# A delta rule with masked exponents and masked copies, unpadded convolutions and packed Fourier tables, in a two-block network on one core

## The chip, the cores and the metric

The kernel runs on one core of one Trainium2 chip. The metric is the device time in microseconds (us). Three runs of the kernel before took 3624.77, 3631.09 and 3634.4 us; their median, 3631.09 us, is the time before.

## The reference, cut to what matters

The program is two networks behind one another, for 512 positions of width 1024, in fp32. Each has two layers. A layer of the first network has two feed-forward parts and a mixer whose outputs are concatenated: latent attention, an mLSTM (with a depthwise convolution of 5 taps) and a Fourier mixer. A layer of the second network has one feed-forward part and a mixer of sliding-window attention, a gated linear recurrence and the gated delta rule (with a depthwise convolution of 4 taps). The change touches three places.

The Fourier mixer takes the real part of a 2-D transform over positions and group channels, and maps it per group:

```
zg = z.reshape(B, S, 4, 64)
y = fftn(zg, axes=(1, 3), norm='ortho').real
out = einsum('bsgc,gce->bsge', y, w).reshape(B, S, 256) + b
```

The delta rule works on chunks; g is a cumulative sum inside a chunk, and T is the inverse of a unit lower triangular matrix:

```
G = cumsum(gc, axis=-1)
L = exp(where(incl, G[..., :, None] - G[..., None, :], -inf))
kb = kc * bc[..., None]
A = where(strict, einsum('bnhtd,bnhsd->bnhts', kb, kc) * L, 0.0)
T = triangular_solve(eye + A, eye, lower=True, unit_diagonal=True)
U = T @ (vc * bc[..., None]);  W = T @ (kb * exp(G)[..., None])
qk = where(incl, einsum('bnhtd,bnhsd->bnhts', qc, kc) * L, 0.0)
# then, chunk after chunk:
v_new = u - w @ state
o = qd @ state + qkc @ v_new
state = gl * state + kd.T @ v_new
```

The convolutions are depthwise, over positions, with zeros outside the sequence: 5 taps centred in the first network, 4 taps that look back in the second, each followed by a SiLU.

## The kernel before, in words

Activations lie with channels on the 128 partitions and the 512 positions along the row. Weights come from HBM in pieces of 128x1024 (512 KB) on SyncE's (SP's) queue, in the order in which they are used. Each is cut into a high and a low part, ScalarE (ACT) writing the high one (line 382) and VectorE (DVE) the low one (line 383), and a product is three matmuls (lines 407 to 409). The weight parts live in two pools of four buffers each, `whi` and `wlo`; a raw piece in a pool of three, `wraw`. PSUM tiles of 128x512 come from two pools of four, `mm` and `mx`.

The program is written as Python generators. `weave` takes a step of each in turn, and the program's order of instructions on each engine follows from that and from a scheduler behind it, which moves instructions by costs of its own. On the chip each engine works its list in order.

In the second network's mixer the order is: gated recurrence with the first projections, then sliding-window attention up to its keys, the six convolutions (their projection's weights are the last to fill `whi` and `wlo`), and then `weave(gdn, swa)`: the delta rule and the attention, step by step, both wanting PE, DVE and ACT. The attention goes by four pairs of heads: scores (line 1127), mask and maximum (1130, 1132), four small operations (1137 to 1140), 8 exponents on ACT (1144), a division by the sum (1146, 1147, 1149), transposes (1164), a copy (1166), values (1173).

The delta rule goes by four blocks of 128 positions (`block`), each for four heads at once, so its tiles are 128x512. For each block: differences of the cumulative sums `ge` (1443) and their exponent (1444); GpSimd (POOL) multiplies that by a strict mask (1448, into `es`); k times k (1452), times beta and `es` (1454, into `am`). POOL masks `am` to its first off-diagonal (1457), DVE subtracts that from the identity (1458, into `xx`), PE transposes it (1461) and ACT copies it (1462, into `xt`). POOL masks `ge` inclusively (1464), for q times k (1467, 1468), which is transposed (1472, 1473). Then come six rounds that double the inverted size: POOL masks `am` to the round's off-diagonal blocks (1479, `gao`), PE multiplies it with `xt` (1482), ACT copies (1483, `zt`), PE multiplies `xx` with that (1487), DVE subtracts it from `xt` (1488), PE transposes (1493) and ACT copies (1494, new `xx`). `es`, `xt`, `am` and `zt` lie in one `whi` and one `wlo` buffer per block.

In the Fourier mixer, `z` is multiplied with a cosine and a sine table of 257 columns each (line 1057: 4 matmuls per table and half of the channels, 2056 bytes of table per partition in each of 4 transfers), copied (1058), and combined with small products (1060, 1061, 1063) in lines 1068 and 1069. The convolution (`conv`) copies its input into a tile of 520 columns whose margins it clears (832, 834), multiplies with the first tap (840) and adds the others (842).

## Time and profile before

| | |
|---|---|
| median of 3 runs | 3631.09 us |
| the profiled execution | 3626.56 us |
| its span, first to last instruction | 3624.7 us |
| PE (matmuls) busy | 3515.3 us, 97% |
| DVE busy | 2015.2 us, 56% |
| ACT busy | 1370.3 us, 38% |
| POOL busy | 239.2 us, 7% |
| mean granted TensorE clock | 0.989 of full speed |

How to read it: a busy PE is not a PE at its peak, since matmuls are pipelined and their ends modelled. L12 is line 12 of the kernel. An arrow in a row reads "output <- inputs"; behind it stand the tile's shape and the number of instructions. "Idle before <- releaser" says how long the engine sat idle in front of a group and what ended that. The chain of waits is followed back from the last instruction; it names at each moment the one engine that the end waited for. The granted clock is a share of 2.4 GHz; 0.5 is the lower of its two levels.

### The profile page before, as it was taken

The numbers are of one execution on the slowest core, as the hardware profiler recorded it, in microseconds if no ns is written. First come the engines' busy times: TensorE is split into PE (matmuls) and PEld (weight loads), VectorE is DVE, ScalarE is ACT, GpSimd is POOL, SyncE is SP. The second block draws the span as 40 slices with busy tenths as digits, with TensorE's granted clock in tenths as the row PEclk, the third lists the DMA queues.
The fourth block names the chain that finished last, engine by engine and source line by source line (L and its number), as shares of the span: only waits on it lengthen the run. The fifth ranks groups of instructions, "written<-read, shape, count | busy, mean of one in ns | idle before, by whom it ended". The sixth has DMA issues, their size and how long they took to land.

```text
span 3624.7 us, 44757 instructions
## 1 busy us (share of the span) xinstructions
PE 3515.3 (97%) x17726; PEld 2914.2 (80%) x17726; DVE 2015.2 (56%) x3084; ACT 1370.3 (38%) x2247; POOL 239.2 (7%) x202
## 2 busy tenths in 40 slices
PE   9999999999999999999999999899999989899999
PEld 7888778888888888778888887688888877788887
DVE  6555665554575545664555676856333476654333
ACT  4223354223342223463223373454222453543221
POOL 0000000000000000000000002430000022500000
PEclk9999999999999999999999999899999999999999
DMA  5443202444424443213444221002333221022332
GB/s 166 143 132 124 86 29 79 134 145 129 127 93 151 134 148 95 77 39 93 140 145 131 92 78 55 25 14 75 105 94 103 77 66 43 1 71 88 101 96 82
DMA packets 105952, 344.75 MB, mean 95 GB/s; under 512 B 11408, under 2 KB 19600, under 8 KB 105744
## 3 DMA queue, kind: packets, MB, share of 16 engines
q1 hardware_dynamic: 105744, 341.89, 29.7%
q8 instruction: 140, 2.29, 0.3%
q14 instruction: 68, 0.56, 0.0%
HBM read 339.75 MB, written 2.10 MB: 94 GB/s over the span
## 4 chain that ended last, share of the span: by engine, by line
PE 84%; DVE 7%; issue 5%; ACT 2%; POOL 1%; DMA 0%; SPq 0%; POOLq 0%; DVEq 0%; ACTq 0%
PE mm L407 24%; PE mm L409 24%; PE mm L408 24%; PE mm L1487 1%; PE mm L1482 1%; PE mm L478 1%; PE mx L969 1%; PE mm L476 1%; PE mm L477 1%; ACT sc L1144 1%; DVE wlo L383 1%; PE mm L810 1%; PE mx L949 1%; DVE sc L1149 1%; DVE hacc L1285 1%
## 5 line engine op out<-in xcount | busy, mean ns | idle before, releaser
L382 ACT CAST whi<-wraw 128x1024 fp32r<-128x1024 f32 (+3 forms) x540 | 552.9, 1028 | 1570.7 <-PE mm L408 1278.7
L407 PE MATMUL mm<-xh,whi 128*128 128x512 f32 (+1 forms) x2784 | 1053.3, 380 | 8.8 <-ACT whi L382 6.3
L408 PE MATMUL mm<-xl,whi 128*128 128x512 f32 (+1 forms) x2784 | 1055.8, 380 | 1.6 <-DVE xl L589 1.5
L409 PE MATMUL mm<-xh,wlo 128*128 128x512 f32 (+1 forms) x2784 | 1055.6, 380 | 0.4 <-DVE wlo L383 0.3
L383 DVE TENSOR_TENSOR wlo<-wraw,whi 128x1024 fp32r<-128x1024 f32 (+3 forms) x540 | 643.1, 1193 | 275.9 <-ACT whi L382 234.0
L407 PEld LDWEIGHTS mm<-xh,whi 128*128 128x128 f32 x2784 | 522.1, 188 | 107.3 <-ACT whi L382 6.3
L409 PEld LDWEIGHTS mm<-xh,wlo 128*128 128x128 f32 x2784 | 524.9, 189 | 100.8 <-DVE wlo L383 3.3
L408 PEld LDWEIGHTS mm<-xl,whi 128*128 128x128 f32 x2784 | 525.0, 189 | 100.3 <-DVE xl L589 2.4
L409 PE MATMUL mm<-hi,wlo 128*128 128x512 f32 (+1 forms) x1390 | 537.5, 387 | 2.1 <-DVE wlo L383 2.1
L407 PE MATMUL mm<-hi,whi 128*128 128x512 f32 (+1 forms) x1390 | 538.6, 388 | 0.2
L408 PE MATMUL mm<-lo,whi 128*128 128x512 f32 (+1 forms) x1390 | 537.5, 387 | 0.0
L409 PEld LDWEIGHTS mm<-hi,wlo 128*128 128x128 f32 x1390 | 261.1, 188 | 61.0 <-DVE wlo L383 4.2
L407 PEld LDWEIGHTS mm<-hi,whi 128*128 128x128 f32 x1390 | 260.9, 188 | 57.3 <-ACT hi L400 1.1
L408 PEld LDWEIGHTS mm<-lo,whi 128*128 128x128 f32 x1390 | 261.1, 188 | 55.9
L659 DVE SCALAR_TENSOR_TENSOR h<-mm,h 128x512 f32<-128x512 f32 x112 | 77.1, 690 | 237.9 <-PE mm L409 237.9
L1595 DVE SCALAR_TENSOR_TENSOR ada<-wraw,cond,ada 128x1024 f32<-128x1024 f32 x84 | 107.8, 1283 | 95.6 <-DMA wraw<-in_ada_w_dram 95.1
L638 DVE TENSOR_TENSOR gl<-mm,rstd 128x512 f32<-128x512 f32 x88 | 60.7, 690 | 154.3 <-PE mm L409 154.3
L637 DVE TENSOR_TENSOR silu<-mm,rstd 128x512 f32<-128x512 f32 x88 | 60.7, 689 | 143.4 <-PE mm L409 143.3
L659 DVE SCALAR_TENSOR_TENSOR h<-mm,mod,h 128x512 f32<-128x512 f32 (+1 forms) x70 | 48.9, 704 | 153.6 <-PE mm L409 153.6
L400 ACT CAST hi<-gl 128x512 fp32r<-128x512 f32 x132 | 82.0, 621 | 103.3 <-DVE gl L640 102.6
L634 DVE TENSOR_TENSOR gl<-silu,mm 128x512 f32<-128x512 f32 x44 | 30.2, 687 | 135.2 <-PE mm L409 135.2
L401 DVE TENSOR_TENSOR lo<-gl,hi 128x512 fp32r<-128x512 f32 x132 | 90.4, 685 | 15.7 <-ACT hi L400 15.7
(498 smaller groups left out, 3761.0 us busy)
## 6 DMA issues: line engine op xcount, KB each, us to landing
wraw<-in_ffn_gate_dram SPq DMA_DIRECT2D x130, 512.0 KB, 3.5
wraw<-in_ffn_up_dram SPq DMA_DIRECT2D x130, 512.0 KB, 4.1
wraw<-in_ada_w_dram SPq DMA_DIRECT2D x96, 512.0 KB, 3.7
wraw<-in_ffn_down_dram SPq DMA_DIRECT2D x96, 448.0 KB, 3.3
wraw<-in_win_f_dram SPq DMA_DIRECT2D x50, 512.0 KB, 3.5
wraw<-in_ffn_down_dram SPq DMA_DIRECT2D x48, 512.0 KB, 3.5
wraw<-in_w_out_dram SPq DMA_DIRECT2D x32, 512.0 KB, 3.5
wraw<-in_win_t_dram SPq DMA_DIRECT2D x16, 512.0 KB, 3.4
```

The lines of the kernel that those rows point to most:

```text
L382: self.nc.scalar.copy(hi[:, s], raw)
L383: self.nc.vector.tensor_tensor(lo[:, s], raw, hi[:, s].bitcast(F32), op=ALU.subtract)
L400: self.nc.scalar.copy(hi, src)
L401: self.nc.vector.tensor_tensor(lo, src, hi.bitcast(F32), op=ALU.subtract)
L407: T.matmul(ps, whi, xhi, start=first, stop=False)
L408: T.matmul(ps, whi, xlo, start=False, stop=False)
L409: T.matmul(ps, wlo, xhi, start=False, stop=last)
L476: T.matmul(ps, xh[:, bs], w[0][:, s], start=k == 0, stop=False)
L637: nc.vector.tensor_tensor(sg, gate_ps, rb, op=ALU.mult)
L638: nc.vector.tensor_tensor(gg, up_ps, rb, op=ALU.mult)
L659: self.nc.vector.scalar_tensor_tensor(h, ps[:, c], scale, h, op0=ALU.mult, op1=ALU.add)
L1595: V.scalar_tensor_tensor(acc, raw, cond[:, k:k + 1], acc, op0=ALU.mult, op1=ALU.add)
```

## The change

Fourier tables: cosines and sines go side by side into one table of 512 columns (257 cosines, 255 sines; the first and last sine column, both zero, are dropped), so each half of the channels needs 4 matmuls of 512 columns, one copy of 512 columns, and one copy of two small products together. The convolution starts with the tap that needs no shift over all 512 columns, and adds each other tap only over the columns where its input exists, so that no margin is kept or cleared. With both, the tiles of the `m` and `l` slots are 2048 bytes per partition; their numbers (16 and 17) stay.

In the delta rule the POOL multiplications go. The exponent's argument is the maximum of the difference and a mask that holds 0 on and below the diagonal and 1e30 above it, so that its exponent is already masked inclusively. `am` is made with minus beta. `xx` and `xt` begin as identities, which a DMA on SP's queue writes from the identity in SBUF into the `whi` buffer of the block (128 partitions, 8 pieces of 512 bytes each). The first off-diagonal is copied over them through a mask by DVE, once from SBUF and once from PSUM. In each round PE multiplies the whole of `am` with `xt`, and DVE copies only the masked part of the product over `xt`.

```
-    m["strict"] = c < r
-    m["incl"] = c <= r
-    for h in LEVELS[::-1]:
-        m[f"off{h}"] = m[f"lv{h}"].T
+    m["later"] = np.where(c <= r, 0.0, -NEG)
+    m["off1"] = m["lv1"].T
...
-    both = np.stack([np.cos(ang), np.sin(ang)])
-    return np.ascontiguousarray(both.reshape(2, NB, P, HALF).transpose(0, 2, 1, 3)).astype(np.float32)
+
+    both = np.concatenate([np.cos(ang), np.sin(ang)[:, 1:HALF - 1]], axis=1)
+    return np.ascontiguousarray(both.reshape(NB, P, SEQ)).astype(np.float32)
...
-        xp = self.t((P, SEQ + 8), name="conv")
-        V.memset(xp[:, 0:left], 0.0)
-        if n - 1 - left:
-            V.memset(xp[:, left + SEQ:n - 1 + SEQ], 0.0)
+        xp = self.t(name="conv")
         if rstd is None:
-            nc.scalar.copy(xp[:, left:left + SEQ], ps)
+            nc.scalar.copy(xp, ps)
         else:
-            V.tensor_tensor(xp[:, left:left + SEQ], ps, rstd, op=ALU.mult)
+            V.tensor_tensor(xp, ps, rstd, op=ALU.mult)
         acc = self.t(name="cacc")
-        V.tensor_scalar(acc, xp[:, 0:SEQ], taps[:, 0:1], 0.0 if bias is None else bias, op0=ALU.mult, op1=ALU.add)
-        for j in range(1, n):
-            V.scalar_tensor_tensor(acc, xp[:, j:j + SEQ], taps[:, j:j + 1], acc, op0=ALU.mult, op1=ALU.add)
+
+        V.tensor_scalar(acc, xp, taps[:, left:left + 1], 0.0 if bias is None else bias, op0=ALU.mult, op1=ALU.add)
+        for j in range(n):
+            if j != left:
+                to, at = slice(max(0, left - j), SEQ - max(0, j - left)), slice(max(0, j - left), SEQ - max(0, left - j))
+                V.scalar_tensor_tensor(acc[:, to], xp[:, at], taps[:, j:j + 1], acc[:, to], op0=ALU.mult, op1=ALU.add)
...
-            ab, mm = self.t((P, 2, HALF), name="fab"), self.t((P, 3, P), name="fm")
+            ab, mm = self.t(name="fab"), self.t((P, 3, P), name="fm")
+            ps = self.ps()
+            for b in range(NB):
+                nc.tensor.matmul(ps, z[:, b, i * P:(i + 1) * P], tabs[b], start=b == 0, stop=b == NB - 1)
+            nc.scalar.copy(ab, ps)
+            ps = self.ps()
             for w in range(2):
-                ps = self.ps()
-                for b in range(NB):
-                    nc.tensor.matmul(ps[:, 0:HALF], z[:, b, i * P:(i + 1) * P], tabs[w][b], start=b == 0, stop=b == NB - 1)
-                nc.scalar.copy(ab[:, w, :], ps[:, 0:HALF])
-                ps = self.ps()
-                nc.tensor.matmul(ps[:, 0:P], cs[:, w, :], bw[:, i, :], start=True, stop=True)
-                nc.scalar.copy(mm[:, w, :], ps[:, 0:P])
-                if w:
-                    nc.scalar.activation(out=mm[:, 2, :], in_=ps[:, 0:P], func=AF.Copy, scale=-1.0)
+                nc.tensor.matmul(ps[:, w * P:(w + 1) * P], cs[:, w, :], bw[:, i, :], start=True, stop=True)
+            nc.scalar.copy(mm[:, 0:2, :], ps[:, 0:2 * P].rearrange("p (a b) -> p a b", a=2))
+            nc.scalar.activation(out=mm[:, 2, :], in_=ps[:, P:2 * P], func=AF.Copy, scale=-1.0)
             t = self.t(name="fy")
             bias = self.vec("fnet_b", l)[:, i:i + 1]
             for back in range(2):
                 ps = self.ps()
-                nc.tensor.matmul(ps[:, 0:HALF], mm[:, 0, :], ab[:, 0, :], start=True, stop=False)
-                nc.tensor.matmul(ps[:, 0:HALF], mm[:, 1 + back, :], ab[:, 1, :], start=False, stop=True)
+                nc.tensor.matmul(ps[:, 0:HALF], mm[:, 0, :], ab[:, 0:HALF], start=True, stop=False)
+                nc.tensor.matmul(ps[:, inner], mm[:, 1 + back, :], ab[:, HALF:SEQ], start=False, stop=True)
...
-        m0, m1, m2 = self.mats("strict", 4), self.mats("off4", 4), self.mats("off64", 1)
-        offs = [m0[:, 2, :], m0[:, 3, :], m1[:, 0, :], m1[:, 1, :], m1[:, 2, :], m1[:, 3, :], m2[:, 0, :]]
+        m0, m1, m2 = self.mats("lv64", 4), self.mats("lv4", 4), self.mats("later", 2)
+
+        lvs = [m1[:, q, :] for q in (2, 1, 0)] + [m0[:, q, :] for q in (3, 2, 1, 0)]
+        later, off1 = m2[:, 0, :], m2[:, 1, :]
         all4 = lambda m: m.unsqueeze(1).to_broadcast([P, 4, P])
+        nb = self.small(sh, "gnb", 2)
+        V.tensor_scalar(nb, beta, -1.0, None, op0=ALU.mult)
...
-                V.tensor_scalar(e[:, h, :], ps[:, h * P:(h + 1) * P], gc[:, b, h:h + 1], 0.0, op0=ALU.subtract, op1=ALU.max)
+                V.scalar_tensor_tensor(e[:, h, :], ps[:, h * P:(h + 1) * P], gc[:, b, h:h + 1], later, op0=ALU.subtract, op1=ALU.max)
             nc.scalar.activation(out=e, in_=e, func=AF.Exp, scale=-1.0)
             r0 = self.wp.tile([P, 2, 4, P], F32, tag="whi", name=self.nm("gm0"))
             r1 = self.wp.tile([P, 2, 4, P], F32, tag="wlo", name=self.nm("gm1"))
-            es, xt, am, zt = r0[:, 0], r0[:, 1], r1[:, 0], r1[:, 1]
-            G.tensor_tensor(es, e, all4(m0[:, 0, :]), op=ALU.mult)
+            xx, xt, am, zt = r0[:, 0], r0[:, 1], r1[:, 0], r1[:, 1]
+            nc.sync.dma_start(out=r0.rearrange("p a b c -> p (a b) c"), in_=self.ident.unsqueeze(1).to_broadcast([P, 8, P]))
             yield
             ps = self.ps()
             for h in range(4):
                 T.matmul(ps[:, h * P:(h + 1) * P], kz[h][:, s], kz[h][:, s], start=True, stop=True)
             for h in range(4):
-                V.scalar_tensor_tensor(am[:, h, :], ps[:, h * P:(h + 1) * P], beta[:, b, h:h + 1], es[:, h, :], op0=ALU.mult, op1=ALU.mult)
+                V.scalar_tensor_tensor(am[:, h, :], ps[:, h * P:(h + 1) * P], nb[:, b, h:h + 1], e[:, h, :], op0=ALU.mult, op1=ALU.mult)
             yield
-            xx = es
-            G.tensor_tensor(xx, am, all4(offs[0]), op=ALU.mult)
-            V.tensor_tensor(xx, all4(self.ident), xx, op=ALU.subtract)
+
             ps = self.ps()
             for h in range(4):
-                T.transpose(ps[:, h * P:(h + 1) * P], xx[:, h, :], self.ident)
-            nc.scalar.copy(xt, p4(ps))
+                T.transpose(ps[:, h * P:(h + 1) * P], am[:, h, :], self.ident)
+            V.copy_predicated(xx, all4(off1).bitcast(I32), am)
+            V.copy_predicated(xt, all4(lvs[0]).bitcast(I32), p4(ps))
             yield
-            G.tensor_tensor(e, e, all4(m0[:, 1, :]), op=ALU.mult)
             ps = self.ps()
             for h in range(4):
                 T.matmul(ps[:, h * P:(h + 1) * P], q[h // 2][:, s], kz[h][:, s], start=True, stop=True)
@@ -1475,17 +1471,15 @@
             yield
 
             for n in range(1, 7):
-                ao = self.t((P, 4, P), name="gao", tag="x")
-                G.tensor_tensor(ao, am, all4(offs[n]), op=ALU.mult)
                 ps = self.ps()
                 for h in range(4):
-                    T.matmul(ps[:, h * P:(h + 1) * P], ao[:, h, :], xt[:, h, :], start=True, stop=True)
+                    T.matmul(ps[:, h * P:(h + 1) * P], am[:, h, :], xt[:, h, :], start=True, stop=True)
                 nc.scalar.copy(zt, p4(ps))
                 yield
                 ps = self.ps()
                 for h in range(4):
                     T.matmul(ps[:, h * P:(h + 1) * P], xx[:, h, :], zt[:, h, :], start=True, stop=True)
-                V.tensor_tensor(xt, xt, p4(ps), op=ALU.subtract)
+                V.copy_predicated(xt, all4(lvs[n]).bitcast(I32), p4(ps))
```

The scheduler's order moves at three places. The first is DVE at the first pair of heads of the attention, in the first layer of the second network (`sc`, `wm`, `wn` are the attention's, `ge` the delta rule's). Before:

```order
L1130 TENSOR_TENSOR sc_17386<-mx_17383,mats_16914 128x512
L1443 TENSOR_SCALAR ge_17394<-mm_17389,gc_17244 128x128
L1132 TENSOR_REDUCE wm_17311<-sc_17386 128x2
L1443 TENSOR_SCALAR ge_17394<-mm_17389,gc_17244 128x128 x3
L1137 TENSOR_TENSOR wm_17311<-wm_17311,srn_16918 128x8
L1443 TENSOR_SCALAR ge_17430<-mm_17425,gc_17244 128x128
L1138 TENSOR_TENSOR wn_17403<-wm_17311,rows 128x8
L1443 TENSOR_SCALAR ge_17430<-mm_17425,gc_17244 128x128
L1139 TENSOR_TENSOR we_17404<-rows,wn_17403 128x8
L1443 TENSOR_SCALAR ge_17430<-mm_17425,gc_17244 128x128
L1140 TENSOR_SCALAR wn_17403<-wn_17403 128x8
L1443 TENSOR_SCALAR ge_17430<-mm_17425,gc_17244 128x128
```

Now:

```order
L1131 TENSOR_TENSOR wm_17265<-wm_17265,srn_16878 128x8
L1124 TENSOR_TENSOR sc_17419<-mx_17416,mats_16874 128x512
L1132 TENSOR_TENSOR wn_17359<-wm_17265,rows 128x8
L1126 TENSOR_REDUCE wm_17395<-sc_17399 128x2
L1133 TENSOR_TENSOR we_17360<-rows,wn_17359 128x8
L1126 TENSOR_REDUCE wm_17395<-sc_17419 128x2
L1134 TENSOR_SCALAR wn_17359<-wn_17359 128x8
L1124 TENSOR_TENSOR sc_17439<-mx_17436,mats_16874 128x512
L1441 SCALAR_TENSOR_TENSOR ge_17350<-mm_17345,gc_17198,mats_17333 128x128 x4
L1441 SCALAR_TENSOR_TENSOR ge_17386<-mm_17381,gc_17198,mats_17333 128x128 x4
L1441 SCALAR_TENSOR_TENSOR ge_17407<-mm_17402,gc_17198,mats_17333 128x128 x4
L1441 SCALAR_TENSOR_TENSOR ge_17427<-mm_17422,gc_17198,mats_17333 128x128 x3
```

The sixteen instructions on `ge` were mixed with the attention's maxima; now the attention's operations come first and the `ge` of all four blocks behind them, with the new mask (`mats`) as an input.

The second is DVE where `xx` and `xt` are made (`gm` are the delta rule's tiles), up to the attention's second division. Before:

```order
L1454 SCALAR_TENSOR_TENSOR gm_3310_17478<-mm_17547,gb_17225,gm_3309_17477 128x128 x4
L1458 TENSOR_TENSOR gm_3289_17400<-base,gm_3289_17400 128x512
L1458 TENSOR_TENSOR gm_3296_17436<-base,gm_3296_17436 128x512
L1458 TENSOR_TENSOR gm_3303_17457<-base,gm_3303_17457 128x512
L1458 TENSOR_TENSOR gm_3309_17477<-base,gm_3309_17477 128x512
L401 TENSOR_TENSOR lo_17624<-mx_17541,hi_17623 128x512
L1130 TENSOR_TENSOR sc_17631<-mx_17628,mats_16914 128x256
L1146 TENSOR_TENSOR wr_17512<-wr_17512,we_17511 128x8
L1130 TENSOR_TENSOR sc_17644<-mx_17641,mats_16914 128x512
L1147 RECIPROCAL wr_17512<-wr_17512 128x8
L1132 TENSOR_REDUCE wm_17627<-sc_17631 128x2
L1149 TENSOR_TENSOR sc_17443<-sc_17443,wr_17512 128x256
```

Now:

```order
L1452 SCALAR_TENSOR_TENSOR gm_3303_17434<-mm_17503,gnb_17335,ge_17427 128x128 x4
L1458 COPY_PREDICATED gm_3282_17356<-mats_17333,gm_3283_17357 128x512
L1459 COPY_PREDICATED gm_3282_17356<-mats_17331,mm_17521 128x512
L1458 COPY_PREDICATED gm_3289_17392<-mats_17333,gm_3290_17393 128x512
L1459 COPY_PREDICATED gm_3289_17392<-mats_17331,mm_17539 128x512
L1458 COPY_PREDICATED gm_3296_17413<-mats_17333,gm_3297_17414 128x512
L1140 TENSOR_TENSOR wr_17468<-wr_17468,we_17467 128x8
L1459 COPY_PREDICATED gm_3296_17413<-mats_17331,mm_17557 128x512
L1141 RECIPROCAL wr_17468<-wr_17468 128x8
L1458 COPY_PREDICATED gm_3302_17433<-mats_17333,gm_3303_17434 128x512
L1143 TENSOR_TENSOR sc_17399<-sc_17399,wr_17468 128x256
```

Four subtractions became eight masked copies, half of them out of PSUM (`mm`), and the second division, which stood behind the attention's next scores, now stands between the last of these copies and ahead of those scores.

The third is SP's queue behind the last weights of the convolutions' projection (`wraw` from `in_win_f`; `wraw` from `in_w_out` belongs to the next stage). Before:

```order
L299 DMA mats_16914<-in_mats_dram 128x256
L392 DMA wraw_18625<-in_w_out_dram 128x1024
L392 DMA wraw_18631<-in_w_out_dram 128x1024
L392 DMA wraw_18637<-in_w_out_dram 128x1024
L299 DMA mats_17375<-in_mats_dram 128x512
L299 DMA mats_17377<-in_mats_dram 128x512
L299 DMA mats_17379<-in_mats_dram 128x128
```

Now:

```order
L298 DMA mats_16874<-in_mats_dram 128x256
L391 DMA wraw_18525<-in_w_out_dram 128x1024
L1446 DMA gm_3282_17356<-base 128x8x128
L391 DMA wraw_18531<-in_w_out_dram 128x1024
L391 DMA wraw_18537<-in_w_out_dram 128x1024
L1446 DMA gm_3289_17392<-base 128x8x128
L1446 DMA gm_3296_17413<-base 128x8x128
L1446 DMA gm_3302_17433<-base 128x8x128
L298 DMA mats_17329<-in_mats_dram 128x512
L298 DMA mats_17331<-in_mats_dram 128x512
L298 DMA mats_17333<-in_mats_dram 128x256
```

The four transfers of the identity stand ahead of the three that bring the masks; each of the four can be issued only when its block's `whi` buffer is free.

## Rows read from the trace of the kernel before

**Rows 1.** The page: engine totals, and the chain that ended last by engine

```profile
PE 3515.3 (97%) x17726; PEld 2914.2 (80%) x17726; DVE 2015.2 (56%) x3084; ACT 1370.3 (38%) x2247; POOL 239.2 (7%) x202
...
PE 84%; DVE 7%; issue 5%; ACT 2%; POOL 1%; DMA 0%; SPq 0%; POOLq 0%; DVEq 0%; ACTq 0%
```

**Rows 2.** Windows: start:end length, busy of PE, PEld, DVE, ACT, POOL, clock, DMA, GB/s

```profile
2335.00:2396.00 61.00, 50.53 (x371) 41.28 (x373) 48.70 (x83) 33.52 (x90) 42.70 (x31) 0.89 0.00 1
2396.00:2441.00 45.00, 45.00 (x427) 44.71 (x426) 15.58 (x22) 22.71 (x42) 5.23 (x9) 1.00 0.01 3
...
3086.00:3147.00 61.00, 50.64 (x372) 41.40 (x374) 48.87 (x83) 33.55 (x90) 42.72 (x31) 0.89 0.00 1
```

**Rows 3.** The chain in order of time, 2334 to 2397 us: start, us, what

```profile
2334.46 5.73 DVE sc L1149 x4
...
2347.00 5.91 DVE gm L1458 x4
2354.93 4.32 PE mm L1467 x24
...
2367.35 4.46 ACT sc L1144 x16
...
2396.50 3.77 PE mm L1487 x32
```

**Rows 4.** Timeline of DVE, first layer: start, us, engine, line, operation, tiles

```profile
2326.65 0.15 DVE L1138 TENSOR_TENSOR wn<-wm,rows 128x8 f32<-128x8 f32 x1
...
2327.32 1.10 DVE L1140 TENSOR_SCALAR wn<-wn 128x8 f32<-128x8 f32 x1
...
2340.12 1.11 DVE L1454 SCALAR_TENSOR_TENSOR gm<-mm,gb,gm 128x128 f32<-128x128 f32 x4
...
2344.00 1.04 DVE L1138 TENSOR_TENSOR wn<-wm,rows 128x8 f32<-128x8 f32 x1
...
2354.98 2.38 DVE L1149 TENSOR_TENSOR sc<-sc,wr 128x256 f32<-128x256 f32 x4
...
2372.90 5.17 DVE L1149 TENSOR_TENSOR sc<-sc,wr 128x256 f32<-128x256 f32 x4
...
2390.29 3.31 DVE L1149 TENSOR_TENSOR sc<-sc,wr 128x256 f32<-128x256 f32 x4
```

**Rows 5.** Timeline of POOL, 2336 to 2364 us, first layer

```profile
2336.26 1.72 POOL L1464 TENSOR_TENSOR ge<-ge,mats 128x512 f32<-128x512 f32 x1
...
2348.96 6.30 POOL L1479 TENSOR_TENSOR gao<-gm,mats 128x512 f32<-128x512 f32 x4
2363.19 1.27 POOL L1479 TENSOR_TENSOR gao<-gm,mats 128x512 f32<-128x512 f32 x1 [7.92 <-DVE wn L1138]
```

**Rows 6.** One line's instructions, ns min/median/max; last row a group: busy us, mean ns

```profile
L1285 DVE COPY_PREDICATED hacc<-mats,mx x56: 701/721/745, 2186.3 to 2977.0; 128x512 f32<-128x512 int32 x56
...
L1488 DVE TENSOR_TENSOR gm<-gm,mm x48: 669/687/690, 2379.2 to 3186.9; 128x512 f32<-128x512 f32 x48
...
L1458 DVE TENSOR_TENSOR gm<-base,gm x8: 936/1752/1756, 2346.9 to 3102.2; 128x512 f32<-128x512 f32 x8
...
L1166 ACT COPY pt<-mx 128x512 f32<-128x512 f32 x12 | 7.1, 588 | 8.4 <-PE mx L1164 8.4
```

**Rows 7.** Timeline of SP's queue, 2267 to 2287 us, and landings in that stretch

```profile
2285.66 1.33 SPq L299 DMA_DIRECT2D mats<-in_mats_dram  x3
...
mats<-in_mats_dram SPq DMA_DIRECT2D x2, 256.0 KB, 4.5
mats<-in_mats_dram SPq DMA_DIRECT2D x1, 64.0 KB, 4.3
```

**Rows 8.** Timeline of PE: end of the convolutions' projection, then the Fourier mixer

```profile
2301.21 0.40 PE L409 MATMUL mm<-xh,wlo 128*128 128x512 f32 x1
...
577.24 1.97 PE L1057 MATMUL mm<-dft,fz 128*128 128x257 f32 x8 [2.15 <-DMA dft<-in_dft_dram]
...
583.22 0.60 PE L714 MATMUL mm<-base,mh 128*128 128x128 f32 x4
```

More of the change, by code (lines that the diff above doesn't have):

```diff
@@ L1042, in fnet @@
         cs = self.mats("dftc", 2)
-        tabs = []
-        for w in range(2):
-            row = []
-            for b in range(0, NB, 2):
-                t = self.t((P, 2, HALF), name="dft")
-                nc.sync.dma_start(out=t, in_=self.d["dft"][w, :, b:b + 2, :])
-                row += [t[:, 0, :], t[:, 1, :]]
-            tabs.append(row)
-        for i in range(2):
-            ab, mm = self.t((P, 2, HALF), name="fab"), self.t((P, 3, P), name="fm")
-            for w in range(2):
-                ps = self.ps()
-                for b in range(NB):
-                    nc.tensor.matmul(ps[:, 0:HALF], z[:, b, i * P:(i + 1) * P], tabs[w][b], start=b == 0, stop=b == NB - 1)
-                nc.scalar.copy(ab[:, w, :], ps[:, 0:HALF])
-                ps = self.ps()
-                nc.tensor.matmul(ps[:, 0:P], cs[:, w, :], bw[:, i, :], start=True, stop=True)
-                nc.scalar.copy(mm[:, w, :], ps[:, 0:P])
-                if w:
-                    nc.scalar.activation(out=mm[:, 2, :], in_=ps[:, 0:P], func=AF.Copy, scale=-1.0)
+        tabs = [self.t(name="dft") for _ in range(NB)]
+        for b in range(NB):
+            nc.sync.dma_start(out=tabs[b], in_=self.d["dft"][b])
+        inner = slice(1, HALF - 1)
+        for i in range(2):
+            ab, mm = self.t(name="fab"), self.t((P, 3, P), name="fm")
+            ps = self.ps()
+            for b in range(NB):
+                nc.tensor.matmul(ps, z[:, b, i * P:(i + 1) * P], tabs[b], start=b == 0, stop=b == NB - 1)
+            nc.scalar.copy(ab, ps)
+            ps = self.ps()
+            for w in range(2):
+                nc.tensor.matmul(ps[:, w * P:(w + 1) * P], cs[:, w, :], bw[:, i, :], start=True, stop=True)
+            nc.scalar.copy(mm[:, 0:2, :], ps[:, 0:2 * P].rearrange("p (a b) -> p a b", a=2))
+            nc.scalar.activation(out=mm[:, 2, :], in_=ps[:, P:2 * P], func=AF.Copy, scale=-1.0)
             t = self.t(name="fy")
```

## The prediction

> **What bounds the kernel now.** I read the page's totals first: PE is busy 97% of the span and holds 84% of the chain, so nothing off PE matters except where PE waits [rows 1]. The windows show where that is among the places that the change touches. In each layer of the second network the delta rule and the attention share a stretch of 61 us (2335 to 2396 in the first, 3086 to 3147 in the second, nearly the same numbers) in which PE is busy for only 50.5 and its granted clock is 0.89; DVE is busy for 48.7 there and POOL for 42.7 [rows 2]. Behind it, from 2396 to 2441, PE is busy all the time at the full clock and DVE a third of it. So the first stretch can shrink and the second cannot, since the change leaves the delta rule's matmuls as many as they were. Between them the two stretches of 61 us have 21 us of idle PE and, at a clock short by 0.11, 2 x 6.7 us of lost clock: 17.2 us a layer is the most that any relief of DVE can bring.
>
> The chain in order of time says what PE waits for: DVE's division (line 1149, 5.73 us), DVE's subtractions from the identity (1458, 5.91 us), then PE itself, then ACT's exponents (1144, 4.46 us), and from 2396 on PE alone [rows 3]. The timelines of DVE and POOL say why these divisions are long. The same four instructions take 5.73 us at 2334 and 5.17 at 2372, but 2.38 at 2355 and 3.31 at 2390 [rows 3, 4]. POOL multiplies through 2336 and from 2349 to 2355.3, and then sits idle for 7.92 us until 2363.2: just there the division is short [rows 5]. Small operations show it too: 0.15 us alone, 1.10 and 1.04 us beside POOL [rows 4]. Work that reads PSUM does not: four of line 1454 take 1.11 us while POOL multiplies [rows 4]. So POOL's 72 multiplications, 36 a layer, lengthen those DVE operations that have their inputs in SBUF.
>
> **The change part by part, one layer of the delta rule.** POOL's work goes, and with it the lengthening: the divisions fall from 5.73 + 5.17 + 3.31 to 3 x 2.38, 7.1 us less; two small operations fall to 0.15, 1.8 us less; smaller ones of the kind I leave out [rows 3, 4]. The four subtractions, 5.9 us, go [rows 3]. That is 14.8 us off DVE.
>
> What DVE gets: eight masked copies of 128x512, four from PSUM in place of ACT's four, four from SBUF. The nearest row is line 1285's masked copy from PSUM, 0.721 us, of which 0.07 lies under its neighbour: 0.65 each, 5.2 us [rows 6]. For the four from SBUF no row exists. Below stands a price of 0 more; above, that of the subtraction they replace, 1.752 beside POOL [rows 6], 4.1 us a layer more. I take 0.65, since POOL is silent there. In the six rounds 24 subtractions of 0.687 become copies of 0.721 [rows 6]; the four that stand in the DVE-bound part cost 0.14 us together, the other twenty end inside PE's full stretch [rows 2], at nothing; if that cover were gone they would cost 0.7 us. The new mask as an input of the sixteen `ge` operations I count at nothing: line 1454 has the same form, one input from PSUM and one from SBUF, and four of it take 1.11 us [rows 4], 0.26 apart. So DVE's net is 14.8 - 5.2 - 0.1 = 9.5 us.
>
> All of these lie on the chain, but the new order gives some back. ACT's first exponents now have an exponent of the delta rule between them, one instruction of some 0.59 us (a row for such a tile [rows 6]), and DVE's division waits for the last. Ahead of the third pair's exponents now stands a copy out of the first round's product, so that ACT waits for that product: 0.59 and about as much for PE. That is 1.8 us, and 7.7 us a layer remain; 15.4 us for two.
>
> The identities: four transfers of 512 KB stand on SP's queue ahead of the three loads of masks. The last waits until the last weights of the convolutions are used up, at 2301.2 plus 0.4 us [rows 8]; before, the mask loads were issued at 2285.7 [rows 7]. Three such loads, 576 KB together, issued within 1.33 us, each landed within 4.5 [rows 7], so I bound one identity by 5.8 us (all of them as one) and from below by 4.3, and the masks behind it land by about 2301.6 + 5.8 + 1.3 + 4.5 = 2313. The first `ge` needs a mask after the small operation at 2327.3 [rows 4], a cover of 14 us; without it every us would be on the chain. The next weights in that queue are used only behind 2396.
>
> The Fourier mixer: the first half of the channels takes from 577.24 to 583.22 [rows 8]. Sixteen matmuls of 257 columns become eight of 512 per layer, the same columns, so that PE gains nothing; but the first copy, 0.588 us for 512 columns [rows 6], can start only behind the last of them, where half of it had run beside PE. Its length, less what PE does on the small products meanwhile, leaves about 0.2 us, four times in the program: 0.7 us more. Its ends are 0 and 4 x 0.588 = 2.4.
>
> The convolutions keep their number of operations; 20 small clears go. Beside PE's full work they count for nothing, at most 1 us. The slots shrink by 32 bytes without becoming more, which moves nothing.
>
> Sum: 15.4 - 0.7 = 14.7 us. The profiled execution took 3626.6 us, 4.5 below the median of the runs shown, so it becomes 3611.9; against the median, which I predict by, 3631.1 - 14.7 = 3616.4 us.
>
> **The rivals.** *PE and ACT take over.* With DVE short, what is late next is PE at its low clock. If it stays at 0.89, only its 10.5 us of idle per layer can go, and of these it still waits once for ACT's 4.46 us of exponents and the 2.38 us of division behind: 3.7 us a layer are left, 6.7 in all after the Fourier term: 3624 us. For it speaks that PE has 50.5 us of work in those 61; against it, that 7.7 is below 10.5.
>
> *More than the sum.* If PE's clock also comes back to its upper level, 17.2 less the 4.46 of the exponents, 12.7 us a layer, 24.8 in all: 3606 us. For it speaks that POOL's results were themselves waited for in places that I did not count; against it, that the exponents stand three times in the chain and I let them count once.
>
> *The lower clock lasts longer: slower than before.* DVE's new order bunches sixteen `ge` operations, and then sixteen of line 1454 and eight copies, each bunch with little for PE between. In the stretch of rows 2 the mean of 0.89 is a mixture of the two levels, 1.2 and 2.4 GHz: some 13 of 61 us at the lower. Work at the lower level takes twice as long, so each 2 us more at it cost 1 us. From 15.4 us more per layer the gain is gone; if the lower level held until 2396, some 53 us instead of 13, the loss would be 20 us a layer against a gain of 7.7: 3631 + 25 = 3656 us. Against it: the matmuls between the bunches come closer together. The Trainium skill (TensorE: Matmul & The Clock Gate, section on HAM oscillation in Part 1) says that a TensorE whose bursts of matmuls alternate with waits falls back to the lower clock again and again. By that rule this rival gets its chance; the 0.89 agrees that it happens here.
>
> *The masks come late.* Should the identities go one after the other at eight times the 4.3 us of the 64 KB load [rows 7], which also moves in pieces of 512 bytes, the masks would land behind 2329 by some 100 us a layer, and the program be 200 us slower. It decides from 14 us of delay on; the three loads that landed together speak against it. The Trainium skill (DMA: Bandwidth & Descriptors, section "Why small descriptors are slow (HBM only)") says that transfers inside SBUF do not suffer from small pieces; no transfer of that kind is in this trace. By that rule this rival falls, so I leave it 1 in 100.
>
> *Nothing that shows.* The longest waits may be ACT's all along, and the smaller slots change nothing: 3631 us.
>
> **How the numbers follow.** The sum 0.55, with a range of its own of 3610 to 3622; more than the sum 0.17; PE and ACT 0.18; nothing 0.04; lower clock 0.05; late masks 0.01. About 0.3%, 10.9 us, is what a measurement of this kernel tells from no change, so faster begins below 3620.2. Faster: 0.48 of the sum's 0.55 and 0.17, 0.65. Within: 0.07 + 0.18 + 0.04 = 0.29. Slower: 0.06. The range reaches from 3603, past the third case and the unknown copies at no price, to 3631, where PE and ACT, the dear copies (8.2 us in all) and no change lie; outside are the two slow rivals and the tails.
>
> **What would show it.** In the changed profile POOL should be almost empty between 2310 and 2441, and all divisions of line 1149 (1143 there) near 2.4 us; the masked copies near 0.72 us from either memory; the stretch from the first division to the full PE some 8 us shorter in each layer, and PE's idle in it near 3 to 5 us. Each Fourier half should show PE waiting about half a us for ACT in front of its combining matmuls. The prediction is wrong if copies from SBUF take over 1 us, if DVE waits for a DMA at its first `ge`, if the granted clock in the stretch falls below 0.8, or if the divisions stay long without POOL.

## The result: 3587.2 us, about three times the forecast's gain

The changed kernel takes 3587.2 us (median of 4 runs, 3583.9 to 3588.5), the kernel before 3632.7 beside it: a ratio of 0.9878 (0.9861 to 0.9895). The profiled executions took 3586.6 and 3626.6 us, 40.0 apart, where the forecast had 14.7 and a range that ended at 3603.

The page after, totals and chain, answers [rows 1]: PE still 97%, POOL's 239.2 us down to 140.5.

```profile
PE 3484.3 (97%) x17694; PEld 2901.8 (81%) x17694; DVE 1989.1 (55%) x3074; ACT 1364.5 (38%) x2231; POOL 140.5 (4%) x130
...
PE 87%; DVE 6%; issue 3%; ACT 2%; POOL 1%; DMA 1%; SPq 0%; POOLq 0%; DVEq 0%; ACTq 0%
```

PE's busy time fell by 31.0 us, and its list of matmuls is the same but for the Fourier mixer's 16 fewer (32 records, two for each). So most of the gain is PE working faster, not waiting less. Where, is told by the starts of one and the same instruction in both traces (us from the span's start):

| place | before | after | lead of after | gained or lost there |
|---|---|---|---|---|
| first Fourier matmul, layer 0 | 577.24 | 574.39 | 2.85 | +2.85 dense matmuls |
| first dense matmul behind it | 589.37 | 589.23 | 0.14 | -2.71 Fourier |
| dense matmul ahead of layer 1's first mixer | 1529.7 | 1522.5 | 7.2 | +7.1 dense |
| a matmul behind its first scores | 1566.6 | 1556.0 | 10.6 | +3.4 one pause of PE (below) |
| first Fourier matmul, layer 1 | 1629.74 | 1619.22 | 10.5 | -0.1 |
| first dense matmul behind it | 1641.86 | 1632.37 | 9.5 | -1.0 Fourier |
| second network, layer 0 | 2195.9 | 2183.7 | 12.2 | +2.7 dense |
| ahead of the delta rule | 2292.4 | 2278.2 | 14.2 | +2.0 another mixer |
| PE full, delta rule's rounds | 2396.50 | 2372.19 | 24.3 | +10.1 delta rule |
| ahead of layer 1's delta rule | 3055.0 | 3027.6 | 27.4 | +3.1 dense |
| PE full there | 3147.47 | 3111.34 | 36.1 | +8.7 delta rule |
| end | 3624.7 | 3584.7 | 40.0 | +3.9 dense |

Some 20 us come from stretches that are mostly dense matmuls (weights times a whole activation), in which the diff moves nothing, 18.8 from the delta rule, 5.4 from two other places; 3.7 are lost in the Fourier mixer.

**The dense matmuls.** The groups of the page, before and then after (busy us, mean ns; `hi` is half of an activation in a slot of tag `l` or `m`, `xh` one in a slot of tag `x`):

```profile
L407 PE MATMUL mm<-xh,whi 128*128 128x512 f32 (+1 forms) x2784 | 1053.3, 380 | 8.8 <-ACT whi L382 6.3
...
L407 PE MATMUL mm<-hi,whi 128*128 128x512 f32 (+1 forms) x1390 | 538.6, 388 | 0.2
```

```profile
L406 PE MATMUL mm<-xh,whi 128*128 128x512 f32 (+1 forms) x2784 | 1053.3, 380 | 9.7 <-ACT whi L381 6.4
...
L406 PE MATMUL mm<-hi,whi 128*128 128x512 f32 (+1 forms) x1390 | 532.5, 384 | 0.2
```

Only the matmuls on `hi` (and `lo`) got shorter. Their rate is read from start to start, since they overlap. In one feed-forward layer before, 61 steps take 14.21 us, 233 ns each; after, 63 take 14.28, 227 ns:

```profile
2599.65 0.40 PE L408 MATMUL mm<-lo,whi 128*128 128x512 f32 x1
...
2613.86 0.40 PE L409 MATMUL mm<-hi,wlo 128*128 128x512 f32 x1
```

```profile
2574.44 0.39 PE L406 MATMUL mm<-hi,whi 128*128 128x512 f32 x1
...
2588.72 0.39 PE L406 MATMUL mm<-hi,whi 128*128 128x512 f32 x1
```

Over all consecutive pairs of such matmuls (some 3820 of 512 columns, steps of 200 to 260 ns) the mean step is 231.8 ns before and 226.9 after. The means on the page, 388 and 384 ns, also hold the narrower matmuls of 256 columns, so they show the change and not the rate. On `xh` and `xl`, whose slots the diff leaves at 2048 bytes, it is 227 in both.

**The delta rule.** Windows from the attention's first division to PE's last pause ahead of its full work, two layers, before and after (columns of [rows 2]):

```profile
2334.46:2390.23 55.77, 44.76 (x319) 36.64 (x319) 45.31 (x79) 29.27 (x82) 38.58 (x28) 0.88 0.00 1
3085.54:3141.22 55.68, 44.86 (x319) 36.75 (x319) 45.42 (x79) 29.27 (x82) 38.49 (x28) 0.88 0.00 1
```

```profile
2321.97:2365.97 44.00, 39.24 (x328) 33.67 (x326) 33.77 (x84) 27.32 (x78) 1.04 (x4) 1.00 0.00 1
3059.90:3105.11 45.21, 40.77 (x328) 35.05 (x327) 33.77 (x84) 27.41 (x78) 1.05 (x4) 0.96 0.00 1
```

The stretch lost 11.8 and 10.5 us. POOL is empty, DVE 11.5 us lighter, PE's idle 11 us down to 4.8 and 4.4, and PE's own work 4 to 5.5 us shorter because the granted clock is 1.00 and 0.96 instead of 0.88. DVE's rows after answer to [rows 4, 6]:

```profile
2321.97 2.22 DVE L1143 TENSOR_TENSOR sc<-sc,wr 128x256 f32<-128x256 f32 x4
...
2327.36 0.16 DVE L1131 TENSOR_TENSOR wm<-wm,srn 128x8 f32<-128x8 f32 x1
...
2329.73 0.74 DVE L1458 COPY_PREDICATED gm<-mats,gm 128x512 f32<-128x512 int32 x1
2330.36 0.73 DVE L1459 COPY_PREDICATED gm<-mats,mm 128x512 f32<-128x512 int32 x1
```

All divisions take 2.2 us. A masked copy starts 0.63 us after the one before, whether its data come from SBUF (1458) or PSUM (1459).

### The profile page after: what moved, and what is told of

Same layout as the page of the kernel before. It is cut to its first block, busy times and chain, and to the rows that moved or that the text cites. A ratio compares the mean times of both kernels' runs of the same rounds, so it can differ in the third digit from the quotient of the medians.

```text
span 3584.7 us, 44503 instructions
## 1 busy us (share of the span) xinstructions
PE 3484.3 (97%) x17694; PEld 2901.8 (81%) x17694; DVE 1989.1 (55%) x3074; ACT 1364.5 (38%) x2231; POOL 140.5 (4%) x130
## 4 chain that ended last, share of the span: by engine, by line
PE 87%; DVE 6%; issue 3%; ACT 2%; POOL 1%; DMA 1%; SPq 0%; POOLq 0%; DVEq 0%; ACTq 0%
PE mm L406 24%; PE mm L408 24%; PE mm L407 24%; PE mm L1481 1%; PE mm L1476 1%; PE mm L476 1%; PE mm L477 1%; PE mm L475 1%; PE mx L968 1%; DVE hacc L1279 1%; DVE wlo L382 1%; PE mm L809 1%; PE mx L948 1%; ACT sc L1138 1%; PE mx L1121 1%
## 5 line engine op out<-in xcount | busy, mean ns | idle before, releaser
L658 DVE SCALAR_TENSOR_TENSOR h<-mm,mod,h 128x512 f32<-128x512 f32 (+1 forms) x70 | 48.9, 704 | 148.7 <-PE mm L408 148.7
L400 DVE TENSOR_TENSOR lo<-gl,hi 128x512 fp32r<-128x512 f32 x132 | 90.5, 686 | 15.4 <-ACT hi L399 15.4
```

Source lines behind the costliest of these rows:

```text
L400: self.nc.vector.tensor_tensor(lo, src, hi.bitcast(F32), op=ALU.subtract)
L658: self.nc.vector.scalar_tensor_tensor(h, ps[:, c], scale, h, op0=ALU.mult, op1=ALU.add)
```

## Experiments: the slots

Theory A: the 2080-byte slots cost the dense matmuls their rate. Rival: the dense part gained from the new order. First the slots alone, put back in the changed kernel (e1) and taken into the kernel before (e2, with the convolutions and tables that go with them), and the delta rule alone (e3):

```diff
-        xp = self.t(name="conv")
+        xp = self.t((P, SEQ + 8), name="conv")[:, 0:SEQ]
-        tabs = [self.t(name="dft") for _ in range(NB)]
+        tabs = [self.t((P, SEQ + 8), name="dft")[:, 0:SEQ] for _ in range(NB)]
```

> The changed kernel with two tiles widened to 520 columns of which 512 are used, so that the slots of the tags l and m are 2080 bytes again; nothing else differs. Theory A (slot size: in the kernel before, matmuls with hi or lo as the moving operand start every 231 ns, in the changed one every 227, while those with xh or xl, whose slots were always 2048 bytes, start every 227 in both; some 4170 of them times 4.2 ns are 17.7 us): back to 231 ns between starts, hi and lo matmuls at a mean of 387 ns, about 17.7 us above the changed kernel, 3605 us against 3587. Theory B (the dense part gained from something else that changed, the order of the instructions or fewer transfers and clears): 227 ns stay, 3587 us.

> The kernel before with the new convolutions and the packed Fourier tables only, so that all slots are 2048 bytes; its delta rule is the old one, with POOL's multiplications. Theory A (slot size): dense matmuls at 227 ns, 17.7 us gained, 3.7 us lost in the Fourier mixer (12.1 to 14.8 and 12.1 to 13.2 us in the two traces), so about 14 us below the kernel before, 3618 us against 3632; its delta stretch stays at 62 us from the first division to the full PE. Theory B (slot size does nothing): the Fourier loss alone, about 3 us above the kernel before.

> The kernel before with the new delta rule only; convolutions, tables and slots of 2080 bytes stay. Theory A (the gain has two independent parts): the delta rule brings what the two traces show from the first division to the full PE, 62.0 to 50.2 us in the first layer and 62.0 to 51.4 in the second, 22.4 us in all: 3610 us; dense matmuls stay at 231 ns. Theory B (the dense part gained by the new delta rule or its order): 17.7 us more, 3592 us. Theory C (the forecast's own sum for the delta rule, 15.4 us): 3617 us.

Measured: e1 3612.7 us, 0.9954 (0.9939 to 0.9969) of before; e2 3614.7, 0.9960 (0.9945 to 0.9975); e3 3612.9, 0.9956 (0.9941 to 0.9971). The steps are 231.7, 226.9 and 231.8 ns. Theory A holds and its rivals fall: the rate goes with the slots alone. e1 lost 25.5 us against the changed kernel (24.9 between the profiled executions); the steps that begin with a matmul on `hi` or `lo` make 18.3 of that, and the rest is a sum of steps of up to 4 us, up and down, in mixers. e3 gained 16.7 us by the medians, nearer to theory C, the forecast's 15.4 for the delta rule, than to theory A's 22.4; between the profiled executions it is 13.6, of which the delta rule's two places have 5.6 each by the table's way of reading (10.1 and 8.7 in the full change). Its stretches are 48.9 and 48.8 us long, at a clock of 0.86:

```profile
2335.26:2384.15 48.89, 43.61 (x318) 36.80 (x319) 33.28 (x82) 27.43 (x79) 1.03 (x4) 0.86 0.00 1
3079.51:3128.29 48.78, 43.52 (x318) 36.70 (x319) 33.25 (x82) 27.42 (x78) 1.05 (x4) 0.86 0.00 1
```

What of the slots counts? The built program gives each buffer's address: the weights start at 320 within 512 bytes, and after the change all slots do, since 2048 is a multiple of 512; before, those of `l` and `m` started 32 bytes further with each slot. An unused tile ahead of the slots moves them all (e4 by 32 bytes, e6 by 704, e12 to e14 by 64, 128 and 256); in e5 it stands ahead of the weights as well:

```diff
+        self.gp = pool(name="shift", bufs=1)
         self.mp = pool(name="mix", bufs=16)
+        self.nc.vector.memset(self.gp.tile([P, 8], F32, name="shim"), 0.0)
```

> The changed kernel with 32 unused bytes ahead of the slots, so that every slot starts 32 bytes further on; the distances between slots stay multiples of 2048. Theory A1 (what costs is that slots start at different places within 2048 bytes, so that consecutive moving operands are not in step): nothing, 227 ns, 3587 us. Theory A2 (what costs is a start that is no multiple of 64 bytes): all matmuls from these slots at 231 ns or more, those with xh and xl too, which would be 17 to 50 us more, 3605 to 3637 us.

> The changed kernel with 32 unused bytes ahead of the weights' buffers and the slots, so that both start 32 bytes further on. In the run with the slots alone moved by 32 bytes the dense matmuls started every 233.3 ns. Theory R (what counts is that the moving operand and the weights start at the same place within 512 bytes; in the changed kernel both start at 320): 227 ns, 3587 us. Theory M (what counts is that a moving operand starts at a multiple of 64 bytes): 233 ns, 3659 us as in the run before.

> The changed kernel with 704 unused bytes between the weights' buffers and the slots, so that every slot starts at a multiple of 2048 bytes and the weights stay at 320 within 512. Theory R (same place within 512 bytes as the weights): the two are out of step, 231 to 233 ns between dense matmuls, 3635 to 3660 us. Theory M (a multiple of 64 bytes): 227 ns, 3587 us; if a larger multiple is better still, below 227 ns and below 3587 us.

> The changed kernel with 64 unused bytes between the weights' buffers and the slots. If the period is 64 bytes: 227 ns between dense matmuls and 3587 us. If it is longer: 231 to 233 ns and 3635 to 3660 us, as with 32 bytes.

> The changed kernel with 128 unused bytes between the weights' buffers and the slots. If the period is 64 or 128 bytes: 227 ns and 3587 us. If it is longer: 231 to 233 ns and 3635 to 3660 us.

> The changed kernel with 256 unused bytes between the weights' buffers and the slots. If the period is 256 bytes or a part of it: 227 ns and 3587 us. If only 512 is free: 231 to 233 ns and 3635 to 3660 us. In the kernel before, matmuls whose operand lay 256 bytes out of step were no quicker than the others (232.7 against 231.7 ns over all), which speaks for the second.

| run | slots less weights, bytes within 512 | step, ns | us | ratio to before |
|---|---|---|---|---|
| changed kernel | 0 | 226.9 | 3587.2 | 0.9878 (0.9861 to 0.9895) |
| e5, both moved by 32 | 0 | 226.9 | 3589.8 | 0.9900 (0.9883 to 0.9916) |
| e14 | 256 | 226.9 | 3587.5 | one run |
| e12 | 64 | 229.0 | 3610.1 | one run |
| e13 | 128 | 232.6 | 3653.4 | one run |
| e6 | 192 | 233.3 | 3655.3 | 1.0078 (1.0063 to 1.0093) |
| e4 | 32 | 233.3 | 3659.3 | 1.0082 (1.0067 to 1.0097) |

The page of e4: `xh` is now slow too, 385 ns instead of 380.

```profile
L408 PE MATMUL mm<-xh,whi 128*128 128x512 f32 (+1 forms) x2784 | 1066.2, 385 | 10.3 <-ACT whi L383 6.8
...
L408 PE MATMUL mm<-hi,whi 128*128 128x512 f32 (+1 forms) x1390 | 539.5, 389 | 0.2
```

e4 refuted A1: equal distances between slots are not enough. e5 and e6 settle it: a start at an odd multiple of 32 is harmless when the weights share it, and a multiple of 2048 does not help when they don't. What decides, where all slots stand at one distance, is where the moving operand starts relative to the weights, and e14 corrects theory R: 256 bytes are as good as 0. e12 met neither of its two expectations: 64 bytes cost 2.1 ns, a third of the worst.

In the kernel before, where the slots of `l` and `m` stand at all sixteen distances, a matmul's own distance does not set its own step. By the program's addresses laid beside the trace, two neighbours that both lie at 0 or 256 start 229.8 ns apart on average (293 pairs), and only inside rows of sixteen such matmuls does the step come down to 226.7 (68 pairs). So neighbours count too. How, and why distance costs anything, no run here shows.

## Experiments: the delta rule

Theory P: POOL's multiplications lengthen DVE's operations. Rival S: DVE's shorter list gained. e7 puts 36 multiplications a layer back on POOL, into a tile that nobody reads; e9 takes POOL's work out of the kernel before and leaves out its masks.

```diff
+        dm = self.t((P, 4, P), name="gdm", tag="x")
+        busy = lambda y: nc.gpsimd.tensor_tensor(dm, y, all4(m0[:, 0, :]), op=ALU.mult)
...
             nc.scalar.activation(out=e, in_=e, func=AF.Exp, scale=-1.0)
+            busy(e)
...
+                busy(am)
                 ps = self.ps()
```

> The changed kernel with 36 multiplications of 128x512 a layer put back on POOL in the delta rule, where the kernel before had its masks; their results go to a tile that nothing reads, so the matmuls, VectorE's operations and all results stay. Theory P (POOL's multiplications beside VectorE made its divisions long, PE waited for these, and its clock fell to 0.89): divisions of 4 to 6 us instead of 2.2 where POOL works, a granted clock below 0.95 in the stretch before the full PE, and that stretch 7 to 12 us a layer longer: 3601 to 3611 us. Theory S (what counts is VectorE's own shorter list of work, the subtractions and masks that went): divisions at 2.2 us, 3587 us.

```diff
-            G.tensor_tensor(es, e, all4(m0[:, 0, :]), op=ALU.mult)
-            G.tensor_tensor(xx, am, all4(offs[0]), op=ALU.mult)
-            V.tensor_tensor(xx, all4(self.ident), xx, op=ALU.subtract)
+            V.tensor_tensor(xx, all4(self.ident), all4(offs[0]), op=ALU.subtract)
-            G.tensor_tensor(e, e, all4(m0[:, 1, :]), op=ALU.mult)
-                G.tensor_tensor(ao, am, all4(offs[n]), op=ALU.mult)
...
-                    T.matmul(ps[:, h * P:(h + 1) * P], ao[:, h, :], xt[:, h, :], start=True, stop=True)
+                    T.matmul(ps[:, h * P:(h + 1) * P], offs[n], xt[:, h, :], start=True, stop=True)
```

> The kernel before without POOL's 72 mask multiplications (left out: the masks on the exponents and on the triangular matrix; its rounds take the constant masks as operands instead, so the delta rule's values are others, while matmuls, VectorE's and ScalarE's operations stay as many, the four subtractions from the identity too). Slots, convolutions and tables are the old ones. Theory P (POOL's work beside VectorE is what the stretch lost): divisions at 2.2 us, subtractions at 0.69 instead of 1.75 us each, the stretch from the first division to PE's last pause 6 to 9 us a layer shorter than its 55.7, so 3611 to 3617 us, as the run with the new delta rule alone (3613). Theory S (the masked copies and VectorE's shorter list are what gained): 3 us a layer or less, 3623 us or more.

e7 took 3627.6 us, 0.9995 (0.9986 to 1.0005) of before: POOL's work alone cost the changed kernel 40 us, 20 to 22 in each stretch, about twice what theory P had expected. One reason can be read from the traces: nothing but POOL uses what e7's multiplications write, and POOL does 14 of them in one row, where the old kernel's come in rows of six at most. Timelines of POOL and DVE, and the windows of the two stretches:

```profile
2336.48 2.62 POOL L1432 TENSOR_TENSOR gdm<-gm,mats 128x512 f32<-128x512 f32 x2
2339.86 21.24 POOL L1432 TENSOR_TENSOR gdm<-gm,mats 128x512 f32<-128x512 f32 x14 [0.76 <-DVE gm L1455]
```

```profile
2337.70 0.34 DVE L1455 SCALAR_TENSOR_TENSOR gm<-mm,gnb,ge 128x128 f32<-128x128 f32 x1
...
2343.36 0.73 DVE L1463 COPY_PREDICATED gm<-mats,mm 128x512 f32<-128x512 int32 x1
...
2346.91 1.28 DVE L1462 COPY_PREDICATED gm<-mats,gm 128x512 f32<-128x512 int32 x1
2348.10 6.47 DVE L1143 TENSOR_TENSOR sc<-sc,wr 128x256 f32<-128x256 f32 x4
```

```profile
2325.31:2391.02 65.71, 48.51 (x335) 41.03 (x335) 54.71 (x93) 28.39 (x79) 48.77 (x39) 0.82 0.00 1
3081.86:3147.43 65.57, 46.82 (x335) 38.96 (x335) 54.30 (x93) 28.59 (x79) 48.76 (x39) 0.87 0.00 1
```

A division of 2.2 us takes 6.47 beside POOL, a masked copy from SBUF 1.28; a masked copy from PSUM (line 1463) keeps its 0.73. e9 took 3608.7 us, 0.9935 (0.9920 to 0.9951), and its stretches, with the old subtractions still in them, are no longer than the changed kernel's:

```profile
2342.09:2386.47 44.38, 40.81 (x319) 34.04 (x319) 31.54 (x80) 28.64 (x82) 1.04 (x4) 0.92 0.00 1
3088.61:3131.88 43.27, 39.75 (x318) 33.17 (x318) 31.54 (x80) 28.64 (x82) 1.05 (x4) 0.96 0.00 1
```

So POOL's work alone takes the delta rule's gain away, and without it the old subtractions do as well as the new copies. That masked copies bring nothing of their own is shown less well: e9 also leaves out waits, since its subtractions and rounds take constant masks and no longer need `am`. The Trainium skill (SBUF — State Buffer, section "Who interferes with whom") says that a VectorE instruction with two inputs in SBUF contends with a GpSimd instruction that reads SBUF, and one with at most one such input, outside the two-port modes, does not; the traces agree, 6.47 us for the divisions, whose inputs both lie in SBUF, and 0.34 for a product that reads PSUM while POOL works (line 1455 in e7), as long as without POOL.

## Experiments: a better version

e8 puts the Fourier mixer's small products ahead of its transforms, and both halves' transforms ahead of the combining matmuls; e10 moves one copy of each block from ScalarE to VectorE; e11 does both.

```diff
-            ab, mm = self.t(name="fab"), self.t((P, 3, P), name="fm")
-            ps = self.ps()
-            for b in range(NB):
-                nc.tensor.matmul(ps, z[:, b, i * P:(i + 1) * P], tabs[b], start=b == 0, stop=b == NB - 1)
-            nc.scalar.copy(ab, ps)
+            mm = self.t((P, 3, P), name="fm")
...
+            mms.append(mm)
+        for i in range(2):
+            ab = self.t(name="fab")
+            ps = self.ps()
+            for b in range(NB):
+                nc.tensor.matmul(ps, z[:, b, i * P:(i + 1) * P], tabs[b], start=b == 0, stop=b == NB - 1)
+            nc.scalar.copy(ab, ps)
+            abs_.append(ab)
+        for i in range(2):
+            ab, mm = abs_[i], mms[i]
...
-                nc.scalar.copy(zt, p4(ps))
+                (V.tensor_copy if n == 1 else nc.scalar.copy)(zt, p4(ps))
```

> The changed kernel with the Fourier mixer's small products ahead of its transforms, and both halves' transforms ahead of the combining matmuls. In the changed kernel PE waits 0.5 us in front of each of the four groups of combining matmuls, and one first transform runs at the lower clock after 1.9 us of idle PE (5.37 us instead of 3.60). Theory F (the packed tables cost 3.7 us by these waits and that clock): the waits go, the products (0.44 us each) run while the tables still land, the lower clock goes: 4 to 6 us less, 3581 to 3583 us. Theory T (the tables' landing sets the start and the clock all the same): 2 us or less, 3585 to 3587 us.

> The changed kernel with the copies out of the first round's products on VectorE in place of ScalarE, so that ScalarE's exponents of the third pair wait for none of them. The forecast's term (this wait costs about 1.2 us a layer): 44.0 and 45.2 us from the first division to PE's last pause become 42.5 to 43 and 44, 3584 to 3585 us. Rival (the exponents themselves are what PE waits for, wherever the copies are): 3587 us, or 1 us more where VectorE's division comes later by the copies.

> The run with the reordered Fourier mixer and the copies of the first round on VectorE together, as the version to beat the changed kernel. If both terms add: 1.8 us (the Fourier run) and 2.4 us (the copies) below the changed kernel, 3583 us. If PE's clock at the stages behind decides, as it took back 4 of the 6 us that the Fourier run had gained: between 3582 and 3588 us.

e8: 3585.2 us, 0.9890 (0.9872 to 0.9908). From the first transform to the first dense matmul behind it 10.7 us instead of 14.8 in layer 0, and 10.6 instead of 13.2 in layer 1; the products (1.1 us for both halves) now run ahead of that, while the tables land. So the mixer became shorter, as theory F had said, but the time is where its rival had put it. By the starts of the same instructions e8 is 5.5 us ahead of the changed kernel behind layer 0's mixer and 5.9 behind layer 1's, but only some 2 at the end. Of what went back, 1.6 us lie near 1541, 2.2 near 2212 and 1.6 near 2291: in the 15 us around each the granted clock is 0.89, 0.77 and 0.77, where the changed kernel has 1.00, 1.00 and 0.89. e10: 3593.4 us, 0.9893 (0.9879 to 0.9908); the stretches are 45.6 and 45.4 us long, not shorter, so the forecast's wait for the products (1.2 us a layer) costs nothing that this copy can give back. e11: 3584.5 us, 0.9871 (0.9854 to 0.9887). The intervals of all three overlap the changed kernel's, so none of them is shown to be faster or slower than it.

## Why the prediction was wrong

**The step that failed** is "The slots shrink by 32 bytes without becoming more, which moves nothing". I took a slot's size for a matter of room. The run with the slots alone undone costs 25.5 us; 18.3 of them are the steps that begin with a matmul on `hi` or `lo`, summed over the trace (904.5 to 922.8 us), the rest lies in the mixers. With it falls "nothing off PE matters except where PE waits": in the dense stretches PE was busy, but not at its best rate. (The one stretch of which I said that it "cannot" shrink, behind the delta rule, did not: from PE's full work to the next dense matmul it takes 44.7 us in both traces.) The page of before had a hint: `hi` at 388 ns and `xh` at 380, with the same weights. It was a weak one, since these means mix two widths and 4 of the 8 ns stay after the change; I did not ask for the rate.

**The delta rule's mechanism was right, and its sum came near where nothing else changed.** Forecast 15.4; e3 gained 16.7 by the medians, 11.2 in the delta rule's two places by its trace. In the full change these places gave 18.8, with the granted clock at 1.00 and 0.96: the rival "more than the sum", 12.7 us a layer, against 11.8 and 10.5 in the windows. In e3 the clock stayed at 0.86. Term by term: divisions 2.22 (forecast 2.38), small operations 0.16 (0.15), masked copies 0.63 apart from either memory (0.65 taken, nothing to 1.75 bounded). DVE became lighter by 11.5 us in its stretch, not by 9.5. Whether the 1.8 us were given back stays open: e10 moved two thirds of the cause to DVE and gained nothing.

**Masks and identities** were hidden as forecast: the identities landed 3.7 us after their issue (median of four), the masks were issued from 2287.84 on and landed in 4.2, far ahead of the first `ge` at 2316.3.

**The convolutions and tables** together moved nothing: e1 has them and e3 has not, at 3612.7 and 3612.9 us; that is a sum, of the packed tables' loss, of the higher clock that the delta rule had in e1 (1.00 and 0.96, as in the changed kernel) and of pauses elsewhere, and no run takes it apart.

**The Fourier term was mis-sized**: 2.0 us, not 0.7 (0 to 2.4), and in the profiled execution 3.7 with the clock. PE's waits, and the first transform after PE's idle:

```profile
574.39 5.37 PE L1051 MATMUL mm<-dft,fz 128*128 128x512 f32 x8 [1.91 <-DMA dft<-in_dft_dram]
579.60 0.61 PE L1055 MATMUL mm<-fw,mats 128*128 128x128 f32 x4
580.77 0.70 PE L1062 MATMUL mm<-fab,fm 128*128 128x257 f32 x2 [0.56 <-ACT fm L1056]
```

```profile
574.00:583.00 9.00, 8.05 (x24) 4.60 (x25) 0.18 (x1) 1.72 (x5) 0.00 (x0) 0.81 0.04 16
583.00:589.00 6.00, 5.49 (x21) 3.23 (x20) 2.70 (x4) 2.79 (x7) 0.00 (x0) 1.00 0.00 0
```

The wait is for the products' copies (`fm`), which now come behind the longer copy of `fab`, 0.56 and 0.51 us for the two halves: 1.0 us a layer, 12.1 to 13.1. The rest, 1.7 us in layer 0, is the clock at 0.81 behind 1.9 us of idle PE, a term that the forecast did not have for this place. It does not belong to the packed tables: with them layer 0's mixer takes 13.1 us in e1, e5 and e7, and with the old ones 13.8 in e3 and 15.1 in e9.

**What stays open.** The 3.4 us at 1530 to 1567 are one pause: PE waits 2.02 us for DVE before and 2.04 after, and only before does the clock fall behind it (the first row and window are before, the second after):

```profile
1545.78 1.92 PE L969 MATMUL mx<-mv,e 128*128 128x65 f32 x8 [2.02 <-DVE e L960]
```

```profile
1538.40 1.11 PE L968 MATMUL mx<-mv,e 128*128 128x65 f32 x8 [2.04 <-DVE e L959]
```

```profile
1533.00:1560.00 27.00, 24.98 (x106) 19.07 (x105) 19.69 (x42) 15.25 (x35) 0.00 (x0) 0.87 0.00 1
```

```profile
1526.00:1550.00 24.00, 21.96 (x110) 17.10 (x109) 19.84 (x42) 15.71 (x35) 0.00 (x0) 1.00 0.00 1
```

Why one pause of 2 us is followed by the lower level and an equal one is not, no run here separates; the same holds for e3's 0.86 against 1.00, and for what e8 gave back. Nor do the parts add: e2 and e3 gain 15.0 and 16.7 us alone, 45.5 together. In the profiled executions 12 of the 13 us that are missing lie in the delta rule's two places, which gave 18.8 in the full change, 11.2 in e3 and lost 4.5 in e2; that the clock makes all of this is not shown.

## What to carry to other kernels

Place the moving operands of matmuls so that they start at the same byte, modulo 256, as the weights, and let no tile's odd size set a slot (shown here for 512 columns of this kernel's split fp32 parts): look for matmuls of one shape, some of which start 1% or 2% further apart than others. Work given to POOL is not free where DVE has two inputs in SBUF; before moving masks there, ask what DVE does at that time. Where a sum of waits is forecast for a PE that pauses, give the clock a term of its own, of the size of what it has lost.

## What the hardware showed that was not expected

- A 128x512 matmul in a dense row starts every 226.9 ns when all moving operands lie 0 or 256 bytes from the weights within 512, every 229.0 at 64, 232.6 at 128, 233.3 at 32 and 192; with all distances mixed, every 231.8. Over the program the worst of these cost 72 us (3659.3 against 3587.2).
- The same PE pause of 2.0 us is followed by a granted clock of 0.87 over 27 us in one kernel and of 1.00 over 24 us in the other.
- A masked copy of 128x512 takes 0.74 us with its data in SBUF and 0.73 with its data in PSUM, and up to 1.28 from SBUF beside POOL.
